# New row groups for the first four bulk loads of a row-wise absolute maximum, and three bulk stores for one

## The chip, the cores and the metric

One core of a Trainium2 chip. The metric is the device time of one execution in microseconds (us), as the median of several. The span, which the profile shows, is some 1.8 us shorter than the time. In the views, DVE is the engine that reduces; SP and ACT here only issue DMAs (a q marks their issuing queue), SP the loads and the tail store, ACT the bulk stores. An issue is the instruction that starts a DMA, and a packet is one run of bytes that a DMA engine moves.

## The reference

```python
def setup_inputs():
    return {"x": np.random.randn(8192, 8192).astype(np.float32)}

def reference(x):
    return np.linalg.norm(x, ord=np.inf, axis=1)      # the largest |x| of each row
```

268.44 MB in, 32 KB out, and one reduction per row.

## The kernel before

Each partition takes whole rows. 24 bulk loads of 8 MB bring two adjacent rows (64 KB) to each of 128 partitions; seven tail tiles follow in smaller and smaller pieces, so that little is left to reduce when the last byte lands. In the bulk, a group of four loads covers 1024 rows, eight per partition. So a load reads 64 KB, skips to 256 KB further on, reads 64 KB for the next partition, and so on (256 KB is its pitch, the distance from one partition's start to the next one's); and a group's results are eight adjacent floats, 32 bytes, per partition.

```python
    # G = 4 loads to a group, B = 2 rows per partition and load, A = 6 groups
    x_b = x[:split].rearrange("(a p n b) c -> a n p (b c)", p=P, a=A, n=G, b=B)
    out_b = out[:split].rearrange("(a p n b) -> p a (n b)", p=P, a=A, n=G, b=B)
    out_t = out[split:].rearrange("(p t) -> p t", p=P)
    ...
    r_bulk = outp.tile([P, A, G * B], F32)
    r_tail = outp.tile([P, n_tail], F32)
    ...
    for a in range(A):
        for n in range(G):
            t = sbuf.tile([P, W + PAD], F32, tag="t")          # 3 buffers
            nc.sync.dma_start(out=t[:, :W], in_=x_b[a, n])
            absmax(r_bulk[:, a, n * B : (n + 1) * B],
                   t[:, :W].rearrange("p (b c) -> p b c", b=B))
    ...                                                         # the tail tiles
    for j, (b, w) in enumerate(LAST):
        ...                                                     # a piece of the last tile
        if j == len(LAST) - 4:
            ins = nc.scalar.dma_start(out=out_b, in_=r_bulk[:])  # the bulk store, from ACT
            after(ins, done, mybir.DependencyClass.Sync)
    nc.sync.dma_start(out=out_t, in_=r_tail[:])                 # the tail store, from SP
    nc.at_finalize(start_first_load_early)
    nc.at_finalize(finish_on_pool)      # POOL waits for all DMAs at the end
```

## Time and profile before

| | before |
|---|---|
| time, median of 6 runs | 627.51 us (627.37 to 627.82) |
| span of the profiled execution | 625.7 us |
| start of the first and of the last bulk reduction | 21.99, 466.70 us |
| issue of the bulk store | 621.73 us |
| issue of the tail store | 624.05 us |

The page's queue lines, the groups, the chain and both ends of the order of time are shown in the prediction. One more view: the stores of the kernel before, with the size of each and the time from its issue to its landing, which is the last of the 16 signals that its DMA engines send (us, last column).

```profile
out_dram<-r_bulk ACTq DMA_DIRECT2D x1, 24.0 KB, 2.0
out_dram<-r_tail SPq DMA_DIRECT2D x1, 8.0 KB, 1.4
```

The tail store lands last, at 625.47, and the span ends 0.3 us after that.

### The profile page before, as it was taken

What the parts mean: (1) busy time and instruction counts of PE and PEld (TensorE: products, weight loads), DVE (VectorE), ACT (ScalarE), POOL (GpSimd) and SP (SyncE); (2) the same over time, 40 slices, a digit from 0 to 9 for tenths busy, and PEclk for the clock granted to TensorE, in tenths of its full rate; (3) what the DMA queues carried; (4) which work ended last, traced back from release to release, by engine and by line L of the source; (5) the groups of instructions that cost most, each with busy time, mean ns of one, the idle gap of its engine ahead of it and who ended that gap; (6) DMA issues with size and microseconds to landing.
All of it is one profiled execution on the core that took longest, in us unless ns stands there. A gap on an engine that the chain in (4) does not pass through costs nothing.

```text
span 625.7 us, 205 instructions
## 1 busy us (share of the span) xinstructions
DVE 552.9 (88%) x67; POOL 0.2 (0%) x4
## 2 busy tenths in 40 slices
DVE  0588988889988889888898888988889999999998
POOL 0000000000000000000000000000000000000000
DMA  9999999999999999999999999999999999999997
GB/s 402 469 402 452 419 452 419 448 423 436 436 419 452 411 461 402 469 402 469 402 469 402 461 411 452 419 448 423 444 413 421 444 425 431 436 425 430 424 422 315
DMA packets 9282, 268.49 MB, mean 429 GB/s; under 512 B 1856, under 2 KB 1856, under 8 KB 3392
## 3 DMA queue, kind: packets, MB, share of 16 engines
q1 hardware_dynamic: 8496, 268.45, 99.5%
q10 hardware_dynamic: 784, 0.02, 0.1%
q14 instruction: 2, 0.02, 0.0%
HBM read 268.44 MB, written 0.03 MB: 429 GB/s over the span
## 4 chain that ended last, share of the span: by engine, by line
DMA 67%; DVE 31%; issue 1%; another core or an unknown queue 0%; DVEq 0%; SPq 0%
DMA t<-in_x_dram 67%; DVE r_bulk L140 24%; DVE part L140 6%; DVE t L140 2%; DVEq L230 0%; DVE r_tail L140 0%; SPq L159 0%
## 5 line engine op out<-in xcount | busy, mean ns | idle before, releaser
L140 DVE TENSOR_REDUCE r_bulk<-t 128x2 f32<-128x16384 f32 x24 | 413.3, 17220 | 69.7 <-DMA t<-in_x_dram 69.7
L140 DVE TENSOR_REDUCE part<-t 128x1 f32<-128x8192 f32 (+20 forms) x28 | 121.5, 4410 | 0.3 <-DMA t<-in_x_dram 0.3
L140 DVE TENSOR_REDUCE t<-t 128x1 f32<-128x1664 f32 (+8 forms) x11 | 16.7, 1576 | 0.2 <-DMA t<-in_x_dram 0.2
L140 DVE TENSOR_REDUCE r_tail<-t 128x1 f32<-128x644 f32 (+1 forms) x2 | 1.5, 814 | 0.0
L137 DVE MEMSET part<- 128x56 f32 x1 | 0.1, 105 | 0.9 <-PEq L219 0.9
L140 DVE TENSOR_REDUCE r_tail<-part 128x14 f32<-128x56 f32 x1 | 0.2, 201 | 0.0
L219 POOL MEMSET const-bfloat16-1.0<- 128x1 bf16 x1 | 0.1, 101 | 0.0
L219 POOL MEMSET const-uint8-127<- 128x1 uint8 x1 | 0.1, 101 | 0.0
L219 POOL MEMSET const-float32-0.0<- 128x1 f32 x1 | 0.1, 98 | 0.2 <-issue 0.2
L219 POOL MEMSET const-float32-1.0<- 128x1 f32 x1 | 0.1, 98 | 0.0
## 6 DMA issues: line engine op xcount, KB each, us to landing
t<-in_x_dram SPq DMA_DIRECT2D x2, 3392.0 KB, 37.2
t<-in_x_dram SPq DMA_DIRECT2D x1, 5376.0 KB, 40.5
t<-in_x_dram SPq DMA_DIRECT2D x1, 4864.0 KB, 32.9
t<-in_x_dram SPq DMA_DIRECT2D x1, 4800.0 KB, 32.9
t<-in_x_dram SPq DMA_DIRECT2D x1, 4672.0 KB, 34.7
t<-in_x_dram SPq DMA_DIRECT2D x3, 1536.0 KB, 36.9
t<-in_x_dram SPq DMA_DIRECT2D x1, 3520.0 KB, 42.7
t<-in_x_dram SPq DMA_DIRECT2D x1, 3328.0 KB, 40.4
```

The lines of the kernel that those rows point to most:

```text
L137: nc.vector.memset(part[:], 0.0)
L140: return nc.vector.reduce_max(out=o, in_=i, axis=X, apply_absolute_value=True)
L219: nc = _bacc.Bacc("TRN2", target_bir_lowering=False, num_devices=1)
```

## The change

The intent is a quicker start: the very first load reads one stretch of 8 MB, with nothing skipped. Groups may now have different sizes, (1, 3, 4, 4, 4, 4, 4) loads. A group of one has two results per partition, a group of three has six; each size gets a store of its own, from the last group size to the first.

```diff
-    G: int = 4,
+    GROUPS: tuple = (1, 3, 4, 4, 4, 4, 4),
...
-    for a in range(A):
-        for n in range(G):
+    runs = []
+    first = 0
+    for n, same in groupby(GROUPS):
+        count = len(list(same))
+        r = slice(first * B, (first + count * n) * B)
+        o = out[r.start * P : r.stop * P]
+        o = o.rearrange("(a p r) -> p a r", a=count, p=P)
+        runs.append((o, r_bulk[:, r].rearrange("p (a r) -> p a r", a=count)))
+        for a in range(count):
+            lo = (first + a * n) * B * P
+            x_g = x[lo : lo + n * B * P].rearrange(
+                "(p n b) c -> n p (b c)", p=P, n=n, b=B
             )
+            for k in range(n):
...                     # load and reduce as before
+        first += count * n
...
-            ins = nc.scalar.dma_start(out=out_b, in_=r_bulk[:])
-            after(ins, done, mybir.DependencyClass.Sync)
+            for o, r in runs[::-1]:
+                ins = nc.scalar.dma_start(out=o, in_=r)
+                after(ins, done, mybir.DependencyClass.Sync)
```

The three stores write 5x128 runs of 32 bytes, 128 runs of 24 bytes, and 128 runs of 8 bytes. In the output, the runs of one group lie side by side.

More of the change, by code (lines that the diff above doesn't have):

```diff
@@ L5 @@
 from contextlib import ExitStack
+from itertools import groupby
 import concourse.bass as bass
@@ L116 @@
     n_tail = B * (len(TAIL) + 1)
-    n_bulk_rows = rows // P - n_tail
-    assert n_bulk_rows % (G * B) == 0
-    A = n_bulk_rows // (G * B)
-    split = n_bulk_rows * P
-    x_b = x[:split].rearrange("(a p n b) c -> a n p (b c)", p=P, a=A, n=G, b=B)
-    out_b = out[:split].rearrange("(a p n b) -> p a (n b)", p=P, a=A, n=G, b=B)
+    n_bulk = sum(GROUPS) * B
+    assert n_bulk == rows // P - n_tail
+    split = n_bulk * P
     x_t = x[split:].rearrange("(p t b) c -> t p (b c)", p=P, b=B)
@@ L132 @@
     assert sum(parts_of) <= PAD
-    r_bulk = outp.tile([P, A, G * B], F32)
+    r_bulk = outp.tile([P, n_bulk], F32)
     r_tail = outp.tile([P, n_tail], F32)
@@ L142, in absmax @@
         )
-    for a in range(A):
-        for n in range(G):
-            t = sbuf.tile([P, W + PAD], F32, tag="t")
-            nc.sync.dma_start(out=t[:, :W], in_=x_b[a, n])
-            absmax(
-                r_bulk[:, a, n * B : (n + 1) * B],
-                t[:, :W].rearrange("p (b c) -> p b c", b=B),
-            )
+    runs = []
[10 more added lines that the diff above has]
+                "(p n b) c -> n p (b c)", p=P, n=n, b=B
+            )
+            for k in range(n):
+                t = sbuf.tile([P, W + PAD], F32, tag="t")
+                nc.sync.dma_start(out=t[:, :W], in_=x_g[k])
+                at = (first + a * n + k) * B
+                absmax(
+                    r_bulk[:, at : at + B],
+                    t[:, :W].rearrange("p (b c) -> p b c", b=B),
+                )
+        first += count * n
     for i, loads in enumerate(TAIL):
```

## The prediction

> **What bounds the kernel now.** I read the views in this order: the page's engines and slices, the DMA queues, the chain that ended last, the waits of the DVE, then the order of time at both ends. The kernel takes the absolute maximum of each of 8192 rows of 8192 floats, so 268.44 MB must come in once, and about 33 KB goes out.
>
> ```profile
> span 625.7 us, 205 instructions
> DVE 552.9 (88%) x67; POOL 0.2 (0%) x4
> ...
> DVE  0588988889988889888898888988889999999998
> ...
> DMA  9999999999999999999999999999999999999997
> ...
> q1 hardware_dynamic: 8496, 268.45, 99.5%
> q10 hardware_dynamic: 784, 0.02, 0.1%
> HBM read 268.44 MB, written 0.03 MB: 429 GB/s over the span
> ```
>
> The load queue (q1) has packets on the 16 DMA engines for 99.5% of the span; the DVE is busy 88%, and its idle time lies in the first three quarters. The next two fences are the costliest groups, and the chain in order of time.
>
> ```profile
> L140 DVE TENSOR_REDUCE r_bulk<-t 128x2 f32<-128x16384 f32 x24 | 413.3, 17220 | 69.7 <-DMA t<-in_x_dram 69.7
> L140 DVE TENSOR_REDUCE part<-t 128x1 f32<-128x8192 f32 (+20 forms) x28 | 121.5, 4410 | 0.3 <-DMA t<-in_x_dram 0.3
> ```
>
> ```profile
> 0.79 40.47 DMA t<-in_x_dram
> ...
> 77.89 40.76 DMA t<-in_x_dram
> ...
> 135.92 40.77 DMA t<-in_x_dram
> ...
> 590.91 21.42 DMA t<-in_x_dram
> ...
> 612.35 9.89 DVE t L140 x8
> 622.25 0.23 issue
> 622.48 0.59 DVE r_tail L140
> ```
>
> One bulk reduction takes 17.22 us, and a new one starts every 19.35 us (in the order of time: 41.28, 60.64, 80.03, ... 466.70), each after about 2.1 us of waiting for its load. 8.389 MB in 19.35 us is 433 GB/s. So the bulk, 24 loads, goes at the pace of the DMA alone. In the tail the DVE catches up with the loads and is then busy nearly without a gap, by design: the tail's loads shrink so that only little is left to reduce after the last byte. I count two engines there, but both start from where the bulk left them.
>
> The two ends are what the change touches.
>
> ```profile
> 0.00 1.80 SPq L147 DMA_DIRECT2D t<-in_x_dram  x3
> ...
> 21.99 17.22 DVE L140 TENSOR_REDUCE r_bulk<-t 128x2 f32<-128x16384 f32 x1 [21.02 <-DMA t<-in_x_dram]
> 41.28 17.22 DVE L140 TENSOR_REDUCE r_bulk<-t 128x2 f32<-128x16384 f32 x1 [2.07 <-DMA t<-in_x_dram]
> ```
>
> ```profile
> 621.73 0.41 ACTq L200 DMA_DIRECT2D out_dram<-r_bulk  x1
> 622.48 1.55 DVE L140 TENSOR_REDUCE r_tail<-t 128x1 f32<-128x644 f32 x2
> 624.05 0.35 SPq L202 DMA_DIRECT2D out_dram<-r_tail  x1
> ```
>
> The first load lands at 21.99, where one load's share at the steady pace is 19.35: the start costs 2.64 us. The trace's records of single packets split that. The first packet begins 1.01 us after the span's start, and about 0.4 us pass from the last packet's end to the DVE's start, neither of which an address should change. In between, the 16 engines start within 0.81 us of each other, and their first packets of 64 KB take 2.80 to 3.23 us (mean 3.03), where nearly every later one takes 2.42. Spreading each packet's bytes evenly over its duration, the load has moved 8.32 MB after 20 us of data, and 433 GB/s would have moved 8.67 MB: 0.8 us lost, all of it in the first 4 us. Of that, 3.03 - 2.42 = **0.61 us** is slow first packets and about 0.2 us the staggered start.
>
> **What the Trainium skill says.** "DMA: Bandwidth & Descriptors", section "Where 436 GB/s comes from", puts the ceiling of the 16 ports at 435.2 GB/s. The trace agrees: 433 GB/s from load 2 on, so no arrangement of addresses can make the steady part quicker. The same page, "Latency and other measured facts", says that copies whose rows lie a large power of two apart in HBM fall behind (207 GB/s at a pitch of 512 KiB, less at more), that padding the pitch restores the rate, and that the cause is only inferred. The kernel before has a pitch of 256 KB in the bulk and runs at 433 GB/s there, so this case shows no such loss except, possibly, in the first 16 packets. "HBM Reference", section "Latency", gives 0.2 us for an HBM access on average and up to 2 us under load; the 0.61 us excess of the first packets would fit a latency as well as a conflict. "DMA: Bandwidth & Descriptors", section "Issuing engines are not separate DMA queues", says that the stores from ACT run on the same 16 engines as the loads; the trace agrees, though nothing collides: the last load packet begins at 622.56 and the bulk store's first at 622.69.
>
> **The change, part by part.**
> (1) Loads. All 24 bulk loads keep their size, count, 64 KB run per partition, and place in the order; the DVE's 67 instructions and the SP's 59 DMA issues are the same. Only HBM addresses move. Load 1 now reads 8 MB of adjacent rows (pitch 64 KB), loads 2 to 4 read with a pitch of 192 KB, loads 5 to 24 and the tail read what they read before. Loads 2 to 4 already ran at 2.42 us a packet; gain 0. Load 1 can gain from its first round of packets alone: at most 0.61 us, if all of its excess came from the pitch. I think that most of it is the time from request to first byte, which nothing hides for an engine's first packet and which the packet before hides for later ones: load 5 is also the first touch of a new 32 MB region, and its packets take 2.42 us. I take a fifth to a half of the excess as saved, 0.12 to 0.3 us, and **0.25 us** as the middle.
> (2) Does a gain at the start reach the end? Yes, in full: every later load waits for an earlier load or for a reduction that waited for one, and the chain goes from load to reduction to load up to the end without a break by anything with its own clock. All later events move by the same amount.
> (3) Stores. One store with 128x6 runs of 32 bytes becomes three: 128x5 of 32, 128 of 24, 128 of 8 bytes. 768 runs become 896, plus 32 more semaphore packets. The one before: issued at 621.73 (0.41 us), packets from 622.69 to about 623.17, landed 2.0 us after issue, at 623.7. After: three issues of about 0.41 us end near 623.0; the third lands 1.4 to 2.0 us (the two stores' times) after its issue at 622.55, at 624.0 to 624.6. The tail store is issued at 624.05 and lands 1.4 us later at 625.4, and the end waits for that. So about 0.9 us of slack remain; cost 0. The semaphore lanes rotate by two, but the added waits of the second and third store are for loads that landed long before.
> Sum: 627.68 - 0.25 + 0 = **627.4 us**.
>
> **The rivals.**
> (A) The slow first packets are pure start-up latency. For it: load 5 starts on fresh rows at full pace, and latencies of this size are usual. Against it: the first packets spread over 0.43 us, which looks like contention. Time: 627.7, no change. About as likely as my middle.
> (B) The 16 engines, each beginning at rows 256 KB times a power of two apart, hinder one another until they drift apart, and contiguous rows cure it wholly. For it: the skill's entry on pitch, and that the rate recovers after one round. Against it: the same pitch at full rate afterwards. Time: 627.1.
> (C) Contiguous rows are worse: 16 engines read inside one 8 MB stretch, and some share one part of the memory. Nothing in the profile speaks for it. A load that lost 10% would add 2 us; 629.7. A chance of 5%.
> (D) The last of three stores lands after the tail store, or its packets delay it. Against it: 0.9 us of slack, and 896 packets of 7 to 9 ns each over 16 engines are under 1 us. Time: up to 628.2. A chance of 7%.
>
> **The range and the chances.** A and B span 627.1 to 627.7; the three runs before span 627.46 to 627.82, so each side gets about 0.2 us of noise, and D some more above: 626.9 to 628.0 should hold it 8 times in 10. Two per cent is 12.5 us, over ten times anything in the sum, and the steady part is at its ceiling, so within 2% has 98%, and each other outcome 1%, for an unforeseen effect of the addresses.
>
> **What would show each step right or wrong.** In the profile after: the first bulk reduction starts at 21.99 less the gain, 21.7 by my middle (21.4 by B, 21.99 by A), and the reductions after it keep their 19.35 us spacing, loads 2 to 4 too. The mean of the first 16 packets falls from 3.03 to about 2.8 us. The bulk still waits 2.1 us per load, the DVE still takes 17.22 us. At the end three ACT issues of some 0.4 us stand beside an otherwise unchanged order, and the tail store is still the last to land. It would be wrong if a load among the first four took other than 19.35 us, which would mean that the pitch sets the rate in the steady part, or if the span after the tail store's issue grew from its 1.65 us, which would mean that the stores reached the path.

## The result, and the profile after

629.66 us, median of 6 runs (629.41 to 629.70), against 627.51: 2.1 us longer. The ratio is 1.0032, with a 95% interval of 1.0019 to 1.0045. That is well within 2%, but outside the predicted range.

First the start, in the order of time of the changed kernel:

```profile
22.03 17.22 DVE L139 TENSOR_REDUCE r_bulk<-t 128x2 f32<-128x16384 f32 x1 [21.06 <-DMA t<-in_x_dram]
...
466.70 17.22 DVE L139 TENSOR_REDUCE r_bulk<-t 128x2 f32<-128x16384 f32 x1 [2.13 <-DMA t<-in_x_dram]
```

The first reduction starts 0.04 us later than before, not earlier, and the last bulk reduction starts at 466.70 in both. The new addresses have neither given nor taken anything in three quarters of the kernel. Then the end, in the same view:

```profile
622.02 1.49 ACTq L215 DMA_DIRECT2D out_dram<-r_bulk  x3
622.76 1.55 DVE L139 TENSOR_REDUCE r_tail<-t 128x1 f32<-128x644 f32 x2
624.34 0.35 SPq L217 DMA_DIRECT2D out_dram<-r_tail  x1
```

The tail store is issued 0.29 us later than before (624.34 against 624.05); but the span ends 3.5 us after that issue, where it was 1.7. The view of the stores' landings says why:

```profile
out_dram<-r_bulk ACTq DMA_DIRECT2D x1, 20.0 KB, 1.9
out_dram<-r_bulk ACTq DMA_DIRECT2D x1, 3.0 KB, 1.6
out_dram<-r_bulk ACTq DMA_DIRECT2D x1, 1.0 KB, 4.3
out_dram<-r_tail SPq DMA_DIRECT2D x1, 8.0 KB, 3.2
```

The smallest store, 1 KB, takes longest to land: 4.3 us. And the tail store, the same 8 KB in the same 64-byte runs as before, takes 3.2 us instead of 1.4. The trace's records of single packets and signals show where in the store the time lies (us from the span's start):

```
                        first packet   last packet ends   first signal   last signal
640 runs of 32 bytes       622.99          623.43            623.77         623.93
128 runs of 24 bytes       623.52          623.72            623.95         624.10
128 runs of  8 bytes       624.01          624.20            625.06         627.33
tail, 64-byte runs         625.18          625.39            626.74         627.51
```

No packet is slow: the engines have sent the 8-byte runs after 0.2 us. What is late are the signals that the writes have landed, up to 3.1 us after the last packet.

### The profile page after: what moved, and what is told of

It reads as the page before. It is cut to its first block, busy times and chain, and to the rows that moved or that the text cites. A ratio compares the mean times of both kernels' runs of the same rounds, so it can differ in the third digit from the quotient of the medians.

```text
span 627.9 us, 207 instructions
## 1 busy us (share of the span) xinstructions
DVE 553.0 (88%) x67; POOL 0.2 (0%) x4
## 4 chain that ended last, share of the span: by engine, by line
DMA 67%; DVE 31%; issue 1%; another core or an unknown queue 0%; DVEq 0%; SPq 0%
DMA t<-in_x_dram 67%; DVE r_bulk L139 24%; DVE part L139 6%; DVE t L139 2%; DVEq L245 0%; DVE r_tail L139 0%; SPq L173 0%
```

## The experiments

I set out with two theories. **S**: the 8-byte store lands late and holds back the tail store. **L**: the new load addresses cost the time. Kernels ran (e1 to e4, e5 to e8, e9 to e11) on three different chips; the kernel before had 627.68, 627.56 and 627.63 us (medians of 7 runs), and every experiment has 4 runs. The changed kernel itself was not run again, so each experiment is held against the kernel before of its own call. The intervals are some 0.9 us wide to either side: they tell a loss of 2 us from none, but not one of 0.2 us. The landing times, read from the same view as above, are set side by side after the last experiment. "Wrong on purpose" means that part of the output is not written or written elsewhere.

### Without the 8-byte store (e1_skip8)

```diff
-            for o, r in runs[::-1]:
+            for o, r in runs[:0:-1]:
```

> The changed kernel without its third store (128 runs of 8 bytes); 256 results stay unwritten, so the result is wrong on purpose. Theory S (the 8-byte store lands late and holds back the tail store): time falls from 629.66 to 627.5-627.9, the tail store lands 1.4 us after its issue again. Theory L (the new load addresses cost the time): stays at 629.4-629.7.

Measured: 627.69 us (627.58 to 627.95), ratio to before 1.0000 (0.9985 to 1.0015).

```profile
out_dram<-r_bulk ACTq DMA_DIRECT2D x1, 3.0 KB, 1.8
out_dram<-r_tail SPq DMA_DIRECT2D x1, 8.0 KB, 1.5
```

All of the loss is gone with 1 KB of output, and the new loads are still there. S stands; L is out for these addresses.

### Old loads, three stores (e2_stores_only)

```diff
-            ins = nc.scalar.dma_start(out=out_b, in_=r_bulk[:])
-            after(ins, done, mybir.DependencyClass.Sync)
+            for o, r in [
+                (out_b[:, 1:], r_bulk[:, 1:]),
+                (out_b[:, 0, B:], r_bulk[:, 0, B:]),
+                (out_b[:, 0, :B], r_bulk[:, 0, :B]),
+            ]:
+                ins = nc.scalar.dma_start(out=o, in_=r)
+                after(ins, done, mybir.DependencyClass.Sync)
```

> The kernel before with its loads untouched and its one bulk store cut into three of the same counts and run lengths (5x128 of 32 bytes, 128 of 24, 128 of 8), here with 32 bytes from one 8-byte run to the next instead of 8. Theory S in the form 'runs of 8 bytes are slow': about 629.6. Theory S in the form 'runs of 8 bytes side by side are slow, because several fall into the same few bytes of memory': 627.5-628.0. Theory L: 627.5.

Measured: 627.63 us (627.34 to 628.30), right result. The same three counts and run lengths cost nothing that 4 runs can show (ratio 1.0000, 0.9985 to 1.0015). So neither three stores nor 8-byte runs are slow as such; what differs is that the 8-byte runs lie 32 bytes apart instead of side by side. They land 2.1 us after their issue.

### The 8-byte store early (e3_early8)

```diff
         first += count * n
+        if n == 1:
+            nc.scalar.dma_start(out=runs[0][0], in_=runs[0][1])
...
-            for o, r in runs[::-1]:
+            for o, r in runs[:0:-1]:
```

> The changed kernel with the 8-byte store issued right after its own reduction (at about 40 us) instead of at the end. Theory S: the late landing is hidden, 627.4-627.9, and its landing still takes 3 us or more. Theory L: 629.6.

Measured: 627.77 us (627.67 to 627.92), right result. Issued at 39.1 us, the store lands 23.5 us later, because its packets take turns with those of the loads, from 42.8 to 60.2 us (which also shows that stores issued by ACT and loads issued by SP share the DMA engines). Its last signal comes 2.4 us after its last data packet, but that is not a slow write: by the trace's records, 10 of its 16 signal packets were sent by 60.21 us and the other 6 only at 62.05 to 62.25, about one load packet (2.42 us) later; the last signal came 0.35 us after the last of them. So the "3 us or more" of the expectation came true for another reason, and nobody waits for this store. This is the changed kernel with its loss mended, and it is level with the kernel before (ratio 1.0002, 0.9985 to 1.0018). No gain of the loads appears from behind the loss, though one of 0.25 us would be lost in this interval.

### Groups of two (e4_groups22)

```diff
-    GROUPS: tuple = (1, 3, 4, 4, 4, 4, 4),
+    GROUPS: tuple = (2, 2, 4, 4, 4, 4, 4),
```

> Groups 2, 2, 4, 4, 4, 4, 4: 128 KB between partitions in the first four loads, and two stores, 5x128 runs of 32 bytes and 2x128 runs of 16 bytes. Theory S with a cost that grows as the run gets shorter: the 16-byte store lands 0.5 to 1.5 us later than a 32-byte one, which the slack of about 0.9 us mostly hides: 627.5-628.5. Theory L: the load addresses cost about as much as in the changed kernel, 629 or more. First 16 packets: mean 3.0-3.1 us if the start is latency, whatever the pitch.

Measured: 628.26 us (628.08 to 628.52), 0.6 us over before, with a ratio whose interval (0.9994 to 1.0024) includes 1. The 16-byte runs side by side land 3.0 us after their issue, which the tail store's later landing hides, as S said. Loads 3 to 5 lost some 0.6 us here: the reductions after them start 19.57, 19.62 and 19.42 us after the one before, instead of 19.35. I can't put that down to the 128 KB between partitions. Loads 1 and 2 have that pitch too and lost nothing (their reductions start at 21.77 and 41.08 us), load 5 has the old addresses, and kernels with the loads of the changed kernel had such losses at 256 KB: up to 19.54 us at loads 8 and 9 of e6, 19.64 at load 5 of e7. The first 16 packets took 3.13 us on average, a little over the expected 3.0 to 3.1.

### Without the 24-byte store (e5_dense_no24)

From here on I ask what makes the 8-byte store late.

```diff
-            for o, r in runs[::-1]:
+            for o, r in [runs[2], runs[0]]:
```

> The changed kernel without its middle store (24-byte runs; 768 results unwritten, wrong on purpose); the 8-byte store follows the first store at once, so some 0.58 us earlier. Theory S: the last of its 16 landings still comes about 3.1 us after its last packet; the end moves up by the 0.58 us only, 628.9-629.3. Theory P (the slow landing comes from three stores in a row, whatever their runs): 627.5-627.9.

Measured: 629.45 us (629.04 to 629.88). The loss stays with two stores, so it isn't the third store that does it, and theory P falls; the time is 0.15 us above the stretch that S expected.

```profile
out_dram<-r_bulk ACTq DMA_DIRECT2D x1, 1.0 KB, 3.0
out_dram<-r_tail SPq DMA_DIRECT2D x1, 8.0 KB, 3.0
```

One detail went otherwise than S said: the 8-byte store's last signal came 1.7 us after its last packet, at 625.32, yet the tail store, whose packets ended at 625.26, got its last signal at 627.22. The hold-up outlasts the store's own signals.

### The 8-byte runs moved apart (e6_apart16, e7_apart32)

```diff
-            for o, r in runs[::-1]:
+            o8 = out[: 4 * P].rearrange("(p r) -> p r", p=P)[:, :B]   # e7: 8 * P
+            for o, r in [runs[2], (o8, r_bulk[:, :B])]:
```

> As the last, but the 128 runs of 8 bytes lie 16 bytes apart instead of 8 (written to the wrong places on purpose). Theory S-near (writes that fall close together wait for one another): about half the neighbours, so the last landing comes about 1.5 us after the last packet, like the 16-byte runs side by side (1.7 us); hidden by the slack: 627.5-628.0. Theory S-size (8 bytes are slow as such): 629.

> As the last, 32 bytes apart. S-near: last landing at most 1.0 us after the last packet (1.0 was seen where 24-byte runs had just been written between them), 627.5-628.0. S-size: 629.

Measured: 627.90 us (627.54 to 628.25) at 16 bytes apart and 627.95 (627.77 to 628.04) at 32. The same 128 runs of 8 bytes, from the same place in the queue as in e5, land in 1.6 us, and the tail store in 1.4. These are the two lines of e6; those of e7 read the same:

```profile
out_dram<-r_bulk ACTq DMA_DIRECT2D x1, 1.0 KB, 1.6
out_dram<-r_tail SPq DMA_DIRECT2D x1, 8.0 KB, 1.4
```

At 16 bytes I had expected half of the lateness; its signals showed none (the last 0.4 us after the last packet).

### Four groups of one (e8_ones)

```diff
-    GROUPS: tuple = (1, 3, 4, 4, 4, 4, 4),
+    GROUPS: tuple = (1, 1, 1, 1, 4, 4, 4, 4, 4),
```

> Groups 1, 1, 1, 1, 4, 4, 4, 4, 4: each of the first four loads takes 8 MB of adjacent rows; the second store has 4x128 runs of 8 bytes side by side, four times as many as in the changed kernel, over 4 KB instead of 1 KB; the result is right. If writes wait for one another within a few dozen bytes, and such places run beside each other: last landing 3-4 us after the last packet as before, time 629-630. If all such writes queue one behind the other: four times as long, about 12 us, time 637-639.

Measured: 629.55 us (629.13 to 629.75), right result. Four times as many 8-byte runs side by side, over 4 KB, cost no more than 128 over 1 KB. So the writes do not all stand in one queue: whatever makes one wait for another is local, and such places work beside each other.

### Runs of 4 bytes, side by side and 8 bytes apart (e9_four_dense, e10_four_apart8)

By now the theory, **N**, was: writes that fall into the same few dozen bytes go one after another; the number per 64 bytes sets the time, about 0.45 us each. Its rivals (not the prediction's of the same letters): **C**, it takes an unbroken row of short runs; **B**, it goes with the bytes.

```diff
-            for o, r in runs[::-1]:
+            o4 = out[: 1 * P].rearrange("(p r) -> p r", p=P)[:, :1]   # e10: 2 * P
+            for o, r in [runs[2], (o4, r_bulk[:, :1])]:
```

> The changed kernel without the middle store and with 128 runs of 4 bytes side by side in place of the 8-byte ones (to the wrong places, half of the results unwritten, on purpose). Theory N (writes into the same 64 bytes go one after another, about 0.45 us each from the first packet on: 8 of them 3.6 us, 4 of them 1.8 us; other stretches of 64 bytes run beside): 16 writes, 7.2 us after the first packet at about 623.4 us, so the span ends near 631 and the time is 632-633.5. Theory C (it is the closed row of short runs, whatever their number in 64 bytes): 629-629.7. Theory B (it goes with the bytes moved, now half): 628-628.7.

> As the last, but the 4-byte runs lie 8 bytes apart, so 8 of them in 64 bytes, with gaps between. Theory N: 8 writes, 3.6 us after the first packet, span end near 627.2, time 628.8-629.5, as with the 8-byte runs side by side. Theory C (gaps free it, as 8-byte runs 16 bytes apart were free): 627.5-628.0.

Measured: 634.59 us (634.06 to 635.12) side by side, the one loss that stands far out (ratio 1.0113, 1.0096 to 1.0130), and 629.14 (628.98 to 629.65) at 8 bytes apart. The landings of the two, side by side first:

```profile
out_dram<-r_bulk ACTq DMA_DIRECT2D x1, 0.5 KB, 7.5
out_dram<-r_tail SPq DMA_DIRECT2D x1, 8.0 KB, 7.9
```

```profile
out_dram<-r_bulk ACTq DMA_DIRECT2D x1, 0.5 KB, 3.1
out_dram<-r_tail SPq DMA_DIRECT2D x1, 8.0 KB, 2.9
```

Half the bytes in twice as dense a row cost 7.0 us over before instead of 1.9 (e5), so B falls. Runs with gaps between them, at the density of the changed kernel (eight to 64 bytes), cost 1.5 us, so C falls. N gave the order and e10's size, but was too low for e9: it said 632 to 633.5.

### The short store first (e11_short_first)

```diff
-            for o, r in runs[::-1]:
+            for o, r in runs:
```

> The changed kernel with its three stores in the reverse order: the 8-byte store first, about 1.0 us earlier; right result. Theory N: its writes are done 3.6 us after the first packet at about 622.9, the end moves up by about 1 us, time 628.4-628.9; the 24- and 32-byte stores land late too where they wait for it on the same DMA engines. If only what comes last counts: 627.6.

Measured: 629.12 us (628.88 to 629.58), right result; 0.2 us above the expected stretch.

```profile
out_dram<-r_bulk ACTq DMA_DIRECT2D x1, 20.0 KB, 4.0
out_dram<-r_bulk ACTq DMA_DIRECT2D x1, 1.0 KB, 3.1
out_dram<-r_bulk ACTq DMA_DIRECT2D x1, 3.0 KB, 2.8
out_dram<-r_tail SPq DMA_DIRECT2D x1, 8.0 KB, 2.8
```

Now the stores behind it are late: the 20 KB of 32-byte runs take 4.0 us instead of 1.9, the 24-byte runs 2.8 instead of 1.6. Issuing the short store 1 us earlier, as seen from the tail store's issue, brings back only 0.5 us.

### The landings side by side

| kernel | short runs, and how many start in 64 bytes | short store lands after its issue, us | tail store lands after its issue, us | time, us |
|---|---|---|---|---|
| before | none under 32 bytes | - | 1.4 | 627.51 to 627.68 |
| e7 | 8 bytes, 32 apart: 2 | 1.6 | 1.4 | 627.95 |
| e2 | 8 bytes, 32 apart: 2, and 2 of 24 bytes | 2.1 | 1.4 | 627.63 |
| e6 | 8 bytes, 16 apart: 4 | 1.6 | 1.4 | 627.90 |
| e4 | 16 bytes side by side: 4 | 3.0 | 1.5 | 628.26 |
| e10 | 4 bytes, 8 apart: 8 | 3.1 | 2.9 | 629.14 |
| e5 | 8 bytes side by side: 8 | 3.0 | 3.0 | 629.45 |
| after | 8 bytes side by side: 8 | 4.3 | 3.2 | 629.66 |
| e8 | 8 bytes side by side: 8, four times as many | 4.8 | 3.1 | 629.55 |
| e9 | 4 bytes side by side: 16 | 7.5 | 7.9 | 634.59 |

From the short store's issue to the tail store's landing, less the 1.03 us to the short store's first packet (as measured in e5), it is 3.4 us in the changed kernel, 3.8 in e5, 3.7 in e10, 3.9 in e8, 4.1 in e11 and 8.7 in e9. Divided by the number of writes that start in the same 64 bytes, that is an estimate of 0.43 to 0.54 us for each. It counts to the tail store's landing; the short store's own signals come earlier, by 1.7 us in e10 and 1.9 in e5.

## Why the prediction was wrong

**The step that failed is (3), the stores.** It said that the third store "lands 1.4 to 2.0 us (the two stores' times) after its issue at 622.55, at 624.0 to 624.6", that "about 0.9 us of slack remain; cost 0". The issue came at 623.06, 0.2 us later than worked out once the 0.29 us shift of this end is taken off, and the packets took 7 to 9 ns each as assumed. The landing took 4.3 us instead of 2.0. I had borrowed the landing time of stores with 32- and 64-byte runs for one with 8-byte runs, and counted only runs and packets; here the time goes with how densely short writes lie. Without that store the time is 627.69; with its runs moved 16 bytes apart (and the 24-byte store left out, which alone left the loss standing in e5), 627.90.

The rest of the step, that the tail store lands 1.4 us after its issue, failed with it: 3.2 us. Why the tail store waits for a store on another queue, to other addresses, is partly told by the Trainium skill, "DMA: Bandwidth & Descriptors", section "Queues, rings and completion order": an engine's signal lands only after all earlier writes of that engine, on any of its queues. The changed kernel agrees: all 16 of the tail store's signals are late, and the last comes 0.2 us after the short store's last. e5 does not quite: there, the tail store was held 1.9 us past the short store's last signal. So here a full count of signals did not mean that the store held nobody up any longer. What exactly stands in the way then is not shown by any run here.

**Rival D named the right place, but not the way, and was too small.** It named "The last of three stores lands after the tail store, or its packets delay it", and gave it 7% and "up to 628.2". Neither half of it came as written: the short store's last signal, 627.33, was still 0.2 us ahead of the tail store's, 627.51, and its packets took 0.2 us. It was the short store's landing that held back the tail store's. Of the profiled span's 2.1 us, 1.75 are the tail store's landing (3.17 us after its issue against 1.42). Its 0.29 us later issue I can't put down to the change: in the eight other profiles with the same loads (e1, e3, e5 to e7, e9 to e11) that issue lies between 623.95 and 624.52, with the 624.05 of before among them, and from the start of the last bulk reduction to that issue it is 157.64 us here, 157.35 before, and 157.14 to 157.80 in all 13 profiles. A loss of one or two tenths by the loads is not excluded by this.

**Rival C gave the measured time, 629.7, by luck.** No load of the changed kernel lost anything; the time alone would have spoken for C, and the two ends of the profile decided against it.

**Step (1), the loads, was too hopeful by its whole 0.25 us.** What rival A foresaw, no change, is what came, and B falls: the first bulk reduction starts between 21.78 and 22.11 us in the nine profiles with the new loads, against 21.99 before and 21.92 in e2. The first 16 packets took 3.13 us on average after, 3.03 before, and between 3.03 and 3.14 in the eight experiments with the same loads; e8, whose first load is the same, had 3.20, and e2, with the old loads, 2.95. Adjacent rows did not shorten the first packets; with only two profiles of the old loads, whether they lengthened them by 0.1 us stays open. That the excess is time to the first byte was argued in the prediction and remains argued; what is shown is that this pitch does not cure it. That loads 2 to 4 keep their 19.35 us held (19.30, 19.37, 19.35).

**Step (2)**, that a shift at the start passes to the end in full, was not tested by the change, since there was no shift. Other profiles tell a part: in e3 and e5 the first bulk reduction started 0.13 and 0.14 us earlier than before, and the last one 0.14 us earlier in both, so the bulk passes a start on in full when no load is slow. The tail does not hand it on as cleanly: their tail stores were issued 0.08 and 0.17 us later than before. Even a gain of 0.25 us would have been hard to see at the end.

**What remains open.** The size of the stretch in which writes wait for one another: I count per 64 bytes, but the counts per 32 or 128 bytes are in the same proportion. Why 16-byte runs side by side are late by their own signals (3.0 us) and 8-byte runs 16 bytes apart are not (1.6), at the same count: those of e6 may have been held unseen, as e5's were in part, and be done by the time the tail store came; and e4 had two sets of 128. Whether it is the writes that count at all, or how many of the 16 DMA engines write into one stretch: an engine has 8 of 128 runs, so more runs to a stretch can also mean more engines there, and no experiment was made to hold one of the two fixed. The trace's packets don't name their engine. And whether the memory or the DMA engines make them wait: the same page, section "Specifications", says that transfers under 512 bytes are done by reading, changing and writing back, which would suit writes that must take turns; but 32-byte runs, just as much under 512 bytes, land in 2.0 us here.

No version tried beats the kernel before: the mended one, e3, is level with it.

## What to carry to other kernels

A store that ends a kernel is paid by its landing, not by its bytes or packets: give each partition's results a long run (those of 24 and 32 bytes landed in 1.6 to 2.0 us here, unless held up by a dense store before them), or spread short ones (8 bytes were free at 16 bytes apart, 4 bytes at 8 apart were not), or issue them long before the end. When a change of layout for the loads also changes the output's layout, work out the run length of every store it leads to, and don't borrow a landing time from a store with longer runs. And when one change alters both ends of a kernel, compare the two ends of the profile before believing the total.

## What the Trainium skill lacked or had wrong

- "DMA: Bandwidth & Descriptors" gives a fixed cost of a DMA and a rule on short transfers, but nothing on how many short writes fall close together. Here, 128 runs of 8 bytes land 1.6 us after issue when 16 or 32 bytes apart and 3.0 to 4.3 us when side by side; 128 runs of 4 bytes side by side, 7.5 us.
- The same page has nothing on a store that still holds up others after its full count of signals. In e5 the count was full at 625.32 us, and the next store on another queue, with its packets sent by 625.26, was signalled in full at 627.22.
- The same page, section "Latency and other measured facts", lists pitches from 512 KiB up as slow. Here 256 KB and 192 KB ran at the full 433 GB/s (19.35 us for 8.389 MB), and 128 KB did so in load 2 of e4 (19.31 us) and not in loads 3 and 4 (up to 19.62), as 256 KB did not in single loads of e6 and e7 (up to 19.64). No page has pitches this small.
